# Split weights of 256 columns two to a buffer, and first weights loaded ahead of operands, in a decoder block of Strassen units

## The chip, the cores and the metric

One Trainium2 chip, one of its cores. The metric is the device time of one launch in microseconds (us).

## The reference

A decoder block on 2048 tokens of width 1024, in float32: RMS norm, one input projection, gated linear attention beside a gated short convolution, output projection, residual, then a SwiGLU feed-forward block (FFN) with residual, and a last norm. The change lies in the FFN, whose hidden width is 2816:

```python
h2 = rmsnorm(x, norm2_g[l])
ffn = (jax.nn.silu(h2 @ w_ffn_gate[l]) * (h2 @ w_ffn_up[l])) @ w_ffn_down[l]
x = x + ffn
```

## The kernel before

**Matmuls.** Activations lie transposed, channels on the 128 partitions and tokens along the row. Every float32 operand of a matmul is split in two: ACT copies the rounded high part (L153) and DVE subtracts it to get the low part (L154). A product takes three matmuls, high by high, high by low and low by high (`product_step`, L381 to L383), each 128x128 by 128x512.

**Units.** `unit` (L385) multiplies a two by two block of weights with a two by two block of activations by seven products in place of eight, after Strassen and Winograd. Its weights come in one DMA into a buffer `raw` with four quarters (A11, A12, A22, A21; `raw_weights`, L351; the pool `rawp` has two such buffers). `unit_weights` (L358) makes the other four factors from them on POOL (GpSimd): s1 (L364), A21 overwritten (L365), A11 overwritten (L366, the factor S2) and A12 overwritten (L371, S4). So the raw buffer comes free only with the last of its splits. Each of the seven factors is then split by `weight_quarter` (L345) into a buffer `wq` that holds high and low of up to 512 columns; the pool `wqp` has four such buffers, each used by one factor, whatever its width. A product keeps its buffer until its last matmul. The products run in the order A11·B11, S1·T1, S2·T2, A12·B21, S3·T3, S4·B22, A22·T4, on PSUM banks that some of them share: ACT copies a bank out (L401), DVE adds others (L405).

**FFN.** The tokens are done in two halves of 1024. For each half `ffn_up` (L904) runs 22 units of 512 columns, gate and up by turns; the operands B11, T1, T2, B21, T3, B22, T4 of the first half are in SBUF (pool `opp`, 28 buffers, tile `op`), those of the second half are loaded by `load_h2` (L895) from DRAM (`shB11_0` and so on, 512 KB each, 28 loads). Silu, the product of gate and up, and the differences that the down projection needs are split and stored to DRAM (`sa_...`). `ffn_down` (L938) takes the hidden channels in groups: the first group of two blocks with weights `wdown_first`, where a factor has 256 columns (four units, 6 matmuls for a product), the later groups of three blocks with weights `wdown` of 384 columns. Four units make one group. The first group copies its products to y (L401); later groups add theirs to y on POOL (L982), and x1, the residual, too (L989). The finished rows of the first half are stored to DRAM (`sx...`).

**Order.** The program is written in one sequence; a tile scheduler decides from it, at build time, the order of each engine's instructions, with semaphores between engines. All loads and stores are issued by SP, in order: what stands behind a waiting load or store on SP waits too. `load_h2` ties its loads behind a raw load of weights: `raw_loads[-2]`, the last but one at that point.

**The three places.** B1 is the boundary from up to down in the first half, B2 the start of the second half, B3 the boundary from up to down in the second half. The prediction uses these names.

Of the kernel before, what the change touches and what calls it, by code (L numbers as in the profile page):

```python
# [51 lines left out]
def tile_hymba_block(ctx, tc, x, xt, win, wa, wgu, wout, wffn, wdown, wdown_first, small, out):  # L52
# [188 lines left out]
    def no_operands():  # L241
        return {b: [] for _, b in PRODUCTS}
# [87 lines left out]
    def plain_unit(src, ops):  # L330
# [11 lines left out]
                us.append((r, j, settled(o, True), False))  # L342
        return us

    def weight_quarter(src):  # L345
        n = src.shape[-1]
        h = wqp.tile([P, 2, PB], F32R, name="wq", tag="wq")[:, :, 0:n]
        split(src, h[:, 0, :], h[:, 1, :])
        return h

    def raw_weights(src):  # L351
        n = src.shape[-1]
        raw = rawp.tile([P, 4 * PB], F32, name="raw", tag="raw")[:, 0 : 4 * n]
        raw = raw.rearrange("p (a n) -> p a n", a=4)
        raw_loads.append(load(raw, src))
        return raw

    def unit_weights(src):  # L358
        raw = raw_weights(src)
        n = src.shape[-1]  # L360
        a11, a12, a22, a21 = [raw[:, i, :] for i in range(4)]
        s1 = rawp.tile([P, PB], F32, name="s1", tag="s1", bufs=1)[:, 0:n]
        w = {"A11": weight_quarter(a11)}
        pool.tensor_tensor(s1, a21, a22, ALU.add)  # L364
        pool.tensor_tensor(a21, a11, a21, ALU.subtract)  # L365
        pool.tensor_tensor(a11, s1, a11, ALU.subtract)  # L366
        w["S1"] = weight_quarter(s1)
        w["S2"] = weight_quarter(a11)
        w["A12"] = weight_quarter(a12)
        w["S3"] = weight_quarter(a21)  # L370
        pool.tensor_tensor(a12, a12, a11, ALU.subtract)  # L371
        w["S4"] = weight_quarter(a12)
        w["A22"] = weight_quarter(a22)
        return w
# [7 lines left out]
        pe.matmul(o[:], wh, xl, start=False, stop=False, skip_group_check=True)  # L382
        return pe.matmul(o[:], wl, xh, start=False, stop=k == n - 1, skip_group_check=True)  # L383

    def unit(src, ops, into=None):  # L385


        w = unit_weights(src)

        def mul(i, o=None):  # L390
            first = o is None
            o = bank() if first else o
            n, m = PRODUCTS[i]
            for k in range(len(ops[m])):
                product_step(o, w[n], ops[m], k, first)
            tick()
            return o

        def copied(name, o, at):
            t = tt(name) if into is None else into[at]  # L400
            act.activation(t[:], o[:], AF.Copy)  # L401
            return t

        def plus(t, o):
            dve.tensor_tensor(t[:], o[:], t[:], ALU.add)  # L405
            return t


        oa = mul(0)
        c11 = copied("c11", oa, (0, 0))  # L410
        ob = mul(1)
        c22 = copied("c22", ob, (1, 1))
        mul(2, oa)
        c12 = copied("c12", oa, (0, 1))
        plus(c11, mul(3))
        mul(4, oa)
        plus(c22, oa)
        mul(5, ob)
        plus(c12, ob)
        mul(6, oa)  # L420
        if into is not None:
            copied("c21", oa, (1, 0))
        return [(0, 0, c11, False), (1, 1, c22, False), (0, 1, c12, False), (1, 0, oa, True)]
# [469 lines left out]
        yield from combine(lambda k, j: s_x1[2 + j][k][:], C_G2, rb, put)  # L893

    def load_h2():  # L895
        ops, loads = no_operands(), raw_loads[-2]
        for _, n in PRODUCTS:
            for k in range(4):
                o = opp.tile([P, 2, PB], F32R, name="op", tag="op")
                with tc.issue_after(loads.ins):  # L900
                    load(o[:].bitcast(F32), s_h2p[n][k][:])
                ops[n].append(o)
        return ops

    def ffn_up(half, ops):
        for m in range(NF // 2):
            us = unit(wffn[2 * m], ops)
            sg = {(r, j): silu(c, p) for r, j, c, p in us}
            for r, j, c, _ in unit(wffn[2 * m + 1], ops):
                s = sg[r, j]  # L910
                dve.tensor_tensor(s[:], c[:], s[:], ALU.mult)
            b11, b12, b21, b22 = [sg[r, j] for r in range(2) for j in range(2)]
            t1, t2, t3, t4 = [bt(n) for n in ("t1", "t2", "t3", "t4")]
            for y, p, q in ((t1, b12, b11), (t2, b22, t1), (t3, b22, b12), (t4, b21, t2)):
                pool.tensor_tensor(y[:], p[:], q[:], ALU.subtract)
            values = [("B11", b11), ("B21", b21), ("B22", b22)]
            if half == 1 and m >= LAST_GROUP:
                values.append(("B12", b12))
            values += [("T1", t1), ("T2", t2), ("T3", t3), ("T4", t4)]
            background.insert(0, split_later(s_act[half][m], values))  # L920
# [17 lines left out]
    def ffn_down(half):  # L938

        y, early = {}, {}  # L940

        def group_op(m, n):
            return early.pop((m, n)) if (m, n) in early else act_op(half, m, n)

        for u, m0 in enumerate(GROUPS):
# [10 lines left out]
            for d0 in range(0, KD, 2):  # L956
                src = wdown[4 * u - 4 + d0 // 2] if u else wdown_first[d0 // 2]
                if u == 0 and d0 == 2:

                    order = [(m, n) for _, n in PRODUCTS for m in range(GROUPS[1], GROUPS[2])]  # L960
                    for m, n in order[:EARLY]:
                        early[m, n] = act_op(half, m, n)
                if u == 0:
                    for d in (d0, d0 + 1):
                        if d < KD - 1:
                            pair = opp.tile([P, 2, PB], F32, name="y", tag="op")
                        for j in range(2):
                            y[d, j] = pair[:, j, :] if d < KD - 1 else bt("y")[:]
                    unit(src, ops, {(r, j): y[d0 + r, j] for r in range(2) for j in range(2)})
                    continue  # L970
                xs = []
                if u < 3:
                    for d in (d0, d0 + 1):
                        xs.append((y[d, u - 1], bt("x1")))
                        load(xs[-1][1][:], s_x1[2 * half + u - 1][d][:])
                if last and half and d0 == KD - 2:
                    last_unit(src, ops, [act_op(half, m, "B12") for m in ms], y, ssq)
                    break
                for r, j, c, p in unit(src, ops):
                    yy = y[d0 + r, j]  # L980
                    eng = dve if p or last and half and r != j else pool
                    eng.tensor_tensor(yy, c[:], yy, ALU.add)  # L982
                    if last and half:
                        sum_squares(ssq[j], yy, j not in begun)
                        begun.add(j)
                    elif last:
                        store(s_x1[2 * half + j][d0 + r][:], yy)
                for yy, x1 in xs:
                    pool.tensor_tensor(yy, x1[:], yy, ALU.add)  # L989
# [107 lines left out]
        ctx.enter_context(tc.tile_pool(name=n, bufs=bufs, reuse_waits="tile"))  # L1097
        for n, bufs in (("fx", 11), ("fo", 3))
    ]
    for half in range(2):  # L1100
        ffn_up(half, load_h2() if half else h2)
        ffn_down(half)
    drain_background()
    for _ in ahead[0]:
        pass
# [103 lines left out]
```

## Time and profile before

| | us |
|---|---|
| median of three runs | 2098.65 |
| the three runs | 2102.15, 2098.65, 2098.31 |
| the profiled execution's own time | 2102.39 |
| span of its profile | 2100.5 |
| mean granted TensorE clock | 0.992 |

| engine | busy, share of the span |
|---|---|
| PE (TensorE) | 97% |
| DVE (VectorE) | 68% |
| ACT (ScalarE) | 48% |
| POOL (GpSimd) | 46% |

The profile is one execution, read by a hardware profiler. A row of a timeline gives the start in us from the span's start, the duration, the engine, the line of the kernel, the operation, output and inputs, the shape, how many such instructions follow one another, and in brackets how long the engine had idled before and what ended it. PEld is TensorE's weight load, which runs beside its matmuls; SPq is SP's queue, where only issues of DMAs are seen. A row of the windows gives, for a stretch of time, its length, the busy time of PE, PEld, DVE, ACT and POOL with the number of instructions, the granted clock (1.00 is full), the busy share of the DMA engines and the GB/s that they moved. An instruction that hangs over a window's edge is counted in both.

### The profile page before, as it was taken

What the parts mean: (1) busy time and instruction counts of PE and PEld (TensorE: products, weight loads), DVE (VectorE), ACT (ScalarE), POOL (GpSimd) and SP (SyncE); (2) the same over time, 40 slices, a digit from 0 to 9 for tenths busy, and PEclk for the clock granted to TensorE, in tenths of its full rate; (3) what the DMA queues carried; (4) which work ended last, traced back from release to release, by engine and by line L of the source; (5) the groups of instructions that cost most, each with busy time, mean ns of one, the idle gap of its engine ahead of it and who ended that gap; (6) DMA issues with size and microseconds to landing.
All of it is one profiled execution on the core that took longest, in us unless ns stands there. A gap on an engine that the chain in (4) does not pass through costs nothing.

```text
span 2100.5 us, 26873 instructions
## 1 busy us (share of the span) xinstructions
PE 2034.6 (97%) x9133; PEld 1649.8 (79%) x9133; DVE 1420.2 (68%) x1983; ACT 1003.2 (48%) x1990; POOL 971.9 (46%) x703
## 2 busy tenths in 40 slices
PE   6999999999999999999999999999999999999996
PEld 4768888877888878788888878787888888877774
DVE  7669786549743786788887665555767766665554
ACT  6555455656542345545545443333545444453344
POOL 3436322222102464465464338774655445436764
PEclk9999999999999999999999999999999999999998
DMA  7359495425686873655646687698444554587673
GB/s 279 129 167 318 128 340 158 149 81 167 205 281 236 325 251 105 236 200 214 223 175 220 236 314 269 234 344 321 159 178 165 192 210 174 213 340 271 259 270 110
DMA packets 189241, 464.43 MB, mean 221 GB/s; under 512 B 19824, under 2 KB 65072, under 8 KB 179504
## 3 DMA queue, kind: packets, MB, share of 16 engines
q1 hardware_dynamic: 189104, 462.72, 61.1%
q8 instruction: 72, 1.18, 0.2%
q14 instruction: 65, 0.53, 0.1%
HBM read 297.49 MB, written 165.15 MB: 220 GB/s over the span
## 4 chain that ended last, share of the span: by engine, by line
PE 74%; DVE 10%; DMA 8%; issue 3%; POOL 3%; ACT 3%; SPq 0%; DVEq 0%; POOLq 0%; ACTq 0%
PE mm L381 22%; PE mm L383 22%; PE mm L382 22%; DVE wq L154 2%; DVE h L508 2%; PE mm L812 1%; DVE op L154 1%; PE mm L813 1%; PE mm L815 1%; DVE so L154 1%; DMA raw<-in_wffn_dram 1%; DMA raw<-in_wdown_dram 1%; DMA op<-shT 1%; PE a_ps L576 1%; DVE c L405 1%
## 5 line engine op out<-in xcount | busy, mean ns | idle before, releaser
L381 PE MATMUL mm<-op,wq 128*128 128x512 f32 x2499 | 981.6, 395 | 17.8 <-ACT wq L153 7.4
L382 PE MATMUL mm<-op,wq 128*128 128x512 f32 x2499 | 976.9, 391 | 0.0
L383 PE MATMUL mm<-op,wq 128*128 128x512 f32 x2499 | 966.4, 392 | 10.4 <-DVE wq L154 9.6
L154 DVE TENSOR_TENSOR wq<-raw,wq 128x512 fp32r<-128x512 f32 (+2 forms) x626 | 527.7, 850 | 333.2 <-ACT wq L153 330.4
L153 ACT ACTIVATE wq<-raw 128x512 fp32r<-128x512 f32 (+2 forms) x626 | 363.5, 587 | 548.6 <-PE mm L383 391.5
L381 PEld LDWEIGHTS mm<-op,wq 128*128 128x128 f32 x2499 | 471.1, 189 | 132.0 <-ACT wq L153 13.5
L383 PEld LDWEIGHTS mm<-op,wq 128*128 128x128 f32 x2499 | 471.1, 189 | 121.2 <-DVE wq L154 22.6
L382 PEld LDWEIGHTS mm<-op,wq 128*128 128x128 f32 x2499 | 471.1, 189 | 97.0 <-issue 1.0
L366 POOL TENSOR_TENSOR raw<-s,raw 128x512 f32<-128x512 f32 (+2 forms) x97 | 127.6, 1316 | 422.6 <-DVE wq L154 402.5
L405 DVE TENSOR_TENSOR c<-mm,c 128x512 f32<-128x512 f32 x267 | 183.0, 685 | 94.4 <-PE mm L383 92.1
L364 POOL TENSOR_TENSOR s<-raw 128x512 f32<-128x512 f32 (+2 forms) x97 | 129.4, 1334 | 205.3 <-DMA raw<-in_wffn_dram 98.7
L371 POOL TENSOR_TENSOR raw<-raw 128x512 f32<-128x512 f32 (+2 forms) x97 | 126.8, 1307 | 129.6 <-DVE wq L154 122.4
L401 ACT ACTIVATE c<-mm 128x512 f32<-128x512 f32 x267 | 155.0, 586 | 39.0 <-PE mm L383 37.7
L794 POOL TENSOR_TENSOR ssx<-ssx,q 128x512 f32<-128x512 f32 x52 | 75.8, 1470 | 158.7 <-ACT q L793 158.5
L365 POOL TENSOR_TENSOR raw<-raw 128x512 f32<-128x512 f32 (+2 forms) x97 | 135.1, 1392 | 4.0
L982 POOL TENSOR_TENSOR y<-c,y 128x512 f32<-128x512 f32 x66 | 98.7, 1497 | 57.3 <-DVE c L405 53.2
L154 DVE TENSOR_TENSOR so<-t,so 128x512 fp32r<-128x512 f32 x100 | 90.7, 913 | 24.4 <-ACT so L153 24.0
L153 ACT ACTIVATE wq<-s 128x512 fp32r<-128x512 f32 (+2 forms) x97 | 56.8, 586 | 98.7 <-PE mm L383 86.0
L812 PE MATMUL mm<-op,wq 128*128 128x512 f32 x256 | 100.9, 395 | 0.0
L813 PE MATMUL mm<-op,wq 128*128 128x512 f32 x256 | 99.8, 390 | 0.0
L154 DVE TENSOR_TENSOR wq<-s,wq 128x512 fp32r<-128x512 f32 (+2 forms) x97 | 84.0, 866 | 17.0 <-ACT wq L153 16.4
L153 ACT ACTIVATE so<-t 128x512 fp32r<-128x512 f32 x100 | 62.5, 626 | 37.8 <-DMA sa_B<-so 16.1
(181 smaller groups left out, 1880.3 us busy)
## 6 DMA issues: line engine op xcount, KB each, us to landing
raw<-in_wffn_dram SPq DMA_DIRECT2D x44, 1024.0 KB, 6.1
sa_T<-so SPq DMA_DIRECT2D x88, 512.0 KB, 4.9
op<-sa_T SPq DMA_DIRECT2D x88, 512.0 KB, 9.4
sa_B<-so SPq DMA_DIRECT2D x69, 512.0 KB, 3.4
op<-sa_B SPq DMA_DIRECT2D x69, 512.0 KB, 9.0
raw<-in_win_dram SPq DMA_DIRECT2D x23, 1024.0 KB, 5.4
raw<-in_wdown_dram SPq DMA_DIRECT2D x24, 768.0 KB, 6.1
sx<-y SPq DMA_DIRECT2D x48, 256.0 KB, 3.3
```

What stands on the lines that cost most here:

```text
L153: last_hi[:] = [act.activation(hi, src, AF.Copy)]
L154: return dve.tensor_tensor(lo, src, hi.bitcast(F32), ALU.subtract)
L364: pool.tensor_tensor(s1, a21, a22, ALU.add)
L365: pool.tensor_tensor(a21, a11, a21, ALU.subtract)
L366: pool.tensor_tensor(a11, s1, a11, ALU.subtract)
L371: pool.tensor_tensor(a12, a12, a11, ALU.subtract)
L381: pe.matmul(o[:], wh, xh, start=first and k == 0, stop=False, skip_group_check=True)
L382: pe.matmul(o[:], wh, xl, start=False, stop=False, skip_group_check=True)
L383: return pe.matmul(o[:], wl, xh, start=False, stop=k == n - 1, skip_group_check=True)
L401: act.activation(t[:], o[:], AF.Copy)
L405: dve.tensor_tensor(t[:], o[:], t[:], ALU.add)
L812: pe.matmul(o[e, j][:], wh, m[:, 0, :], start=k == 0, stop=False)
```

## The change

It has three parts and adds or removes no matmul, split, addition or transfer.

1. `weight_quarter` gives a whole `wq` buffer only to factors of more than 256 columns. Narrower ones, which only the first group of the down projection has, go two to a buffer; the second half of a buffer is kept in `beside` for the next narrow factor, across units too.
2. `ffn_down` loads the first weights of its first group at its start, ahead of the operands of that group.
3. The first gate weights of the second half are loaded ahead of `load_h2`, whose 28 operand loads are now tied behind the last raw load, which is that one.

The loop over the two halves is written out.

```diff
@@ -342,9 +342,19 @@
                 us.append((r, j, settled(o, True), False))
         return us
 
+    beside = []
+
     def weight_quarter(src):
         n = src.shape[-1]
-        h = wqp.tile([P, 2, PB], F32R, name="wq", tag="wq")[:, :, 0:n]
+        if n > PB // 2:
+            beside.clear()
+            h = wqp.tile([P, 2, PB], F32R, name="wq", tag="wq")[:, :, 0:n]
+        elif beside:
+            h = beside.pop()
+        else:
+            both = wqp.tile([P, 2, PB], F32R, name="wq", tag="wq")
+            beside.append(both[:, :, PB // 2 : PB // 2 + n])
+            h = both[:, :, 0:n]
         split(src, h[:, 0, :], h[:, 1, :])
         return h
 
@@ -355,8 +365,8 @@
         raw_loads.append(load(raw, src))
         return raw
 
-    def unit_weights(src):
-        raw = raw_weights(src)
+    def unit_weights(src, raw=None):
+        raw = raw_weights(src) if raw is None else raw
         n = src.shape[-1]
         a11, a12, a22, a21 = [raw[:, i, :] for i in range(4)]
         s1 = rawp.tile([P, PB], F32, name="s1", tag="s1", bufs=1)[:, 0:n]
@@ -382,10 +392,10 @@
         pe.matmul(o[:], wh, xl, start=False, stop=False, skip_group_check=True)
         return pe.matmul(o[:], wl, xh, start=False, stop=k == n - 1, skip_group_check=True)
 
-    def unit(src, ops, into=None):
-
-
-        w = unit_weights(src)
+    def unit(src, ops, into=None, raw=None):
+
+
+        w = unit_weights(src, raw)
 
         def mul(i, o=None):
             first = o is None
@@ -893,7 +903,7 @@
         yield from combine(lambda k, j: s_x1[2 + j][k][:], C_G2, rb, put)
 
     def load_h2():
-        ops, loads = no_operands(), raw_loads[-2]
+        ops, loads = no_operands(), raw_loads[-1]
         for _, n in PRODUCTS:
             for k in range(4):
                 o = opp.tile([P, 2, PB], F32R, name="op", tag="op")
@@ -902,9 +912,9 @@
                 ops[n].append(o)
         return ops
 
-    def ffn_up(half, ops):
+    def ffn_up(half, ops, raw=None):
         for m in range(NF // 2):
-            us = unit(wffn[2 * m], ops)
+            us = unit(wffn[2 * m], ops, raw=None if m else raw)
             sg = {(r, j): silu(c, p) for r, j, c, p in us}
             for r, j, c, _ in unit(wffn[2 * m + 1], ops):
                 s = sg[r, j]
@@ -938,6 +948,7 @@
     def ffn_down(half):
 
         y, early = {}, {}
+        raw = raw_weights(wdown_first[0])
 
         def group_op(m, n):
             return early.pop((m, n)) if (m, n) in early else act_op(half, m, n)
@@ -966,7 +977,8 @@
                             pair = opp.tile([P, 2, PB], F32, name="y", tag="op")
                         for j in range(2):
                             y[d, j] = pair[:, j, :] if d < KD - 1 else bt("y")[:]
-                    unit(src, ops, {(r, j): y[d0 + r, j] for r in range(2) for j in range(2)})
+                    into = {(r, j): y[d0 + r, j] for r in range(2) for j in range(2)}
+                    unit(src, ops, into, raw if d0 == 0 else None)
                     continue
                 xs = []
                 if u < 3:
@@ -1097,9 +1109,11 @@
         ctx.enter_context(tc.tile_pool(name=n, bufs=bufs, reuse_waits="tile"))
         for n, bufs in (("fx", 11), ("fo", 3))
     ]
-    for half in range(2):
-        ffn_up(half, load_h2() if half else h2)
-        ffn_down(half)
+    ffn_up(0, h2)
+    ffn_down(0)
+    raw = raw_weights(wffn[0])
+    ffn_up(1, load_h2(), raw)
+    ffn_down(1)
     drain_background()
     for _ in ahead[0]:
         pass
```

Line numbers behind the first part grow by 10: L381, L401 and L405 become L391, L411 and L415.

Up to B1 every engine's order is as before. What moves there on ACT, at the end of the second and the start of the third unit of the first down group. `raw_11028` before and `raw_11021` now is the third unit's weights, `y` are copies of the second unit's products, `so` are splits of activations on their way to DRAM. Before:

```order
L401 ACTIVATE y_10821<-mm_10850 128x512
L153 ACTIVATE wq_10952<-raw_10930 128x256
L153 ACTIVATE wq_10955<-raw_10930 128x256
L401 ACTIVATE y_10928<-mm_10958 128x512
L153 ACTIVATE so_10984<-t2_10785 128x512
L401 ACTIVATE y_10929<-mm_10958 128x512
L153 ACTIVATE so_11003<-t3_10786 128x512
L153 ACTIVATE wq_11031<-raw_11028 128x256
L153 ACTIVATE wq_11037<-s1_11030 128x256
```

Now:

```order
L153 ACTIVATE wq_10946<-raw_10927 128x256
L411 ACTIVATE y_10926<-mm_10963 128x512
L411 ACTIVATE y_10823<-mm_10847 128x512
L411 ACTIVATE y_10925<-mm_10951 128x512
L153 ACTIVATE wq_11024<-raw_11021 128x256
L153 ACTIVATE wq_11032<-raw_11021 128x256
L153 ACTIVATE wq_11024<-s1_11023 128x256
L411 ACTIVATE y_10926<-mm_10951 128x512
L153 ACTIVATE so_10977<-t2_10785 128x512
L153 ACTIVATE wq_11032<-raw_11021 128x256
```

The split of the third unit's A11 stood behind the copy of the second unit's last product and a split of activations; it now stands ahead of both, and two factors share a buffer (`wq_11024`).

On SP at the same place, before:

```order
L145 DMA op_10926<-sa0_2_T2_241 128x1024
L148 DMA sa0_10_B21_302<-so_10884 128x1024
L148 DMA sa0_10_B22_303<-so_10902 128x1024
L145 DMA raw_11028<-in_wdown_first_dram 128x1024
L148 DMA sa0_10_T1_304<-so_10965 128x1024
L145 DMA raw_11111<-in_wdown_first_dram 128x1024
```

Now:

```order
L145 DMA op_10923<-sa0_2_T2_241 128x1024
L145 DMA raw_11021<-in_wdown_first_dram 128x1024
L148 DMA sa0_10_B21_302<-so_10881 128x1024
L148 DMA sa0_10_B22_303<-so_10899 128x1024
L148 DMA sa0_10_T1_304<-so_10958 128x1024
```

The third unit's raw load went ahead of two stores of activations. B3 moves in the same way.

On SP at B2, the start of the second half, before (`shB11` are the four parts of the operand B11, `sx` rows of the first half, stored and reloaded as `y` for the last norm):

```order
L145 DMA op_12651<-shB11_0_412 128x1024
L148 DMA sx0_1_169<-y_10821 128x512
L148 DMA sx1_3_179<-y_10929 128x512
L148 DMA sx1_2_178<-y_10928 128x512
L148 DMA sx0_3_171<-y_10929 128x512
L145 DMA op_12653<-shB11_1_413 128x1024
L145 DMA y_12810<-sx0_1_169 128x512
L145 DMA y_12902<-sx0_2_170 128x512
L145 DMA op_12655<-shB11_2_414 128x1024
L145 DMA op_12657<-shB11_3_415 128x1024
L145 DMA y_12962<-sx0_3_171 128x512
L145 DMA raw_12707<-in_wffn_dram 128x2048
```

Now:

```order
L148 DMA sx0_3_171<-y_10926 128x512
L145 DMA y_12948<-sx0_3_171 128x512
L145 DMA raw_12637<-in_wffn_dram 128x2048
L145 DMA op_12639<-shB11_0_412 128x1024
L148 DMA sx0_4_172<-y_11019 128x512
L145 DMA op_12641<-shB11_1_413 128x1024
L145 DMA op_12643<-shB11_2_414 128x1024
L145 DMA op_12645<-shB11_3_415 128x1024
L148 DMA sx1_4_180<-y_11019 128x512
L145 DMA op_12647<-shT1_0_416 128x1024
```

The four loads of B11 stood ahead of the first gate weights of the second half and now stand behind them, around two stores.

## The prediction

> **What bounds the kernel now.** I read the page first, then TensorE's waits, then windows about each place where the order of instructions changes, and last the timelines of single engines there.
>
> The page, busy time by engine and the chain of waits:
>
> ```profile
> PE 2034.6 (97%) x9133; PEld 1649.8 (79%) x9133; DVE 1420.2 (68%) x1983; ACT 1003.2 (48%) x1990; POOL 971.9 (46%) x703
> ...
> PE 74%; DVE 10%; DMA 8%; issue 3%; POOL 3%; ACT 3%; SPq 0%; DVEq 0%; POOLq 0%; ACTq 0%
> ```
>
> TensorE is busy for 97% of the span and the change takes no matmul away. So it can only win the time in which TensorE waits, or runs slower than it can. What TensorE waits for in the Strassen units most (us in total, times, longest):
>
> ```profile
> PE mm L383 <- DVE wq L154: 9.6, 7, 2.7
> PE mm L381 <- ACT wq L153: 7.4, 7, 1.8
> PE mm L381 <- ACT c L401: 6.6, 7, 2.6
> ```
>
> These three are 24 us in the whole program; the change reaches only those at three boundaries. Windows (length; PE, PEld, DVE, ACT, POOL busy with counts; granted clock; DMA share; GB/s) give an undisturbed stretch, the first boundary from up to down (B1), the start of the second half (B2), the second boundary from up to down (B3), the stage behind B3, and parts of them:
>
> ```profile
> 1100.00:1180.00 80.00, 80.00 (x355) 66.24 (x354) 55.48 (x71) 41.10 (x73) 37.02 (x26) 1.00 0.46 165
> 1205.57:1240.99 35.42, 32.99 (x134) 25.45 (x132) 23.52 (x38) 16.85 (x38) 14.75 (x16) 0.95 0.74 286
> 1423.76:1467.12 43.36, 40.12 (x166) 31.81 (x165) 19.40 (x25) 15.71 (x27) 16.55 (x13) 0.96 0.84 332
> 1850.03:1893.79 43.76, 41.27 (x175) 32.02 (x174) 32.43 (x51) 23.17 (x52) 18.57 (x20) 1.00 0.84 325
> 1893.79:1938.69 44.90, 43.07 (x187) 34.44 (x186) 23.94 (x33) 15.67 (x31) 28.52 (x24) 1.00 0.73 269
> 1215.09:1230.69 15.60, 13.19 (x56) 9.71 (x54) 9.40 (x17) 6.40 (x15) 3.52 (x5) 1.00 0.85 328
> 1232.30:1235.80 3.50, 3.50 (x10) 2.68 (x10) 1.79 (x4) 1.70 (x5) 2.65 (x4) 0.55 0.62 250
> 1457.60:1461.00 3.40, 3.40 (x9) 2.60 (x9) 2.67 (x3) 1.24 (x3) 1.27 (x1) 0.54 0.71 239
> 1876.40:1879.80 3.40, 3.40 (x16) 2.73 (x16) 2.67 (x5) 2.52 (x6) 2.55 (x4) 1.00 0.73 300
> ```
>
> The first row sets the floor: 80.00 us for 354 weight loads (one for each matmul) is 0.226 us a matmul. A window's length less its count times 0.226 is what is lost there: B1 35.42 − 132 × 0.226 = 5.6 us, B2 6.1, B3 4.4, the stage behind B3 2.9. Together that is 19 us, the most that these places hold. The profiled execution took 2102.39 us (span 2100.5, so 1.9 around it), 3.74 more than the median of 2098.65, so a gain read from it may hold terms that the median runs don't have.
>
> **The waits that fall.** TensorE's timeline at the boundaries (start, duration, what ended the idle time ahead):
>
> ```profile
> 1227.51 0.50 PE L381 MATMUL mm<-op,wq 128*128 128x512 f32 x1 [0.79 <-DVE y L405]
> ...
> 1230.69 0.50 PE L381 MATMUL mm<-op,wq 128*128 128x512 f32 x1 [1.51 <-ACT wq L153]
> ...
> 1454.60 0.50 PE L381 MATMUL mm<-op,wq 128*128 128x512 f32 x1 [1.50 <-DMA op<-shT]
> ...
> 1457.25 0.74 PE L381 MATMUL mm<-op,wq 128*128 128x512 f32 x1 [1.69 <-ACT c L401]
> ...
> 1875.14 0.50 PE L381 MATMUL mm<-op,wq 128*128 128x512 f32 x1 [1.51 <-ACT wq L153]
> ...
> 1930.18 0.50 PE L381 MATMUL mm<-op,wq 128*128 128x512 f32 x1 [1.76 <-ACT wq L153]
> ```
>
> *B1.* The 1.51 us at 1230.69 is the third unit's A11 weight. Its history, read backwards on ACT, SP and DVE:
>
> ```profile
> 1211.27 0.42 ACT L153 ACTIVATE wq<-raw 128x256 fp32r<-128x256 f32 x1 [1.88 <-PE mm L383]
> ...
> 1230.23 0.41 ACT L153 ACTIVATE wq<-raw 128x256 fp32r<-128x256 f32 x1
> ```
>
> ```profile
> 1213.96 1.47 SPq L148 DMA_DIRECT2D sa_B<-so  x2
> 1216.02 0.33 SPq L145 DMA_DIRECT2D raw<-in_wdown_first_dram  x1
> ```
>
> ```profile
> 1215.01 0.95 DVE L154 TENSOR_TENSOR wq<-raw,wq 128x256 fp32r<-128x256 f32 x1
> ```
>
> ```profile
> raw<-in_wdown_first_dram SPq DMA_DIRECT2D x1, 512.0 KB, 9.6
> ```
>
> A split at 1211.27 had to wait 1.88 us for TensorE, since all four wq buffers were in use. So the first unit's last split ended at 1215.01 + 0.95 = 1215.96; only then was its raw buffer free, and the third load went out at 1216.02, behind two stores. It took 9.6 us, to 1225.6. On ACT its split, at 1230.23, stands behind the copy of the second unit's last product (the order of ACT shown with the change). With eight quarters in the four buffers all seven of a unit fit, so the first unit's splits do not wait for its products. The 1.88 is gone and the load leaves SP ahead of the two stores, by my estimate at 1216.02 less the stores' 1.47 and the wait's 1.88, so 1212.7, landing 9.6 later, 1222.3; and the order puts the split ahead of the copy. What is late next is only the 0.79 wait at 1227.51, a DVE addition between two products on one bank: it is in no buffer's hands and I leave it. The price of the 1.51 wait: the wait itself, a refill, and the clock behind it. Refill: in 1215.09 to 1230.69 15.60 − 54 × 0.226 = 3.4 us are lost and 15.60 − 13.19 = 2.4 are idle, so 1.0 goes to slower matmuls about two waits, 0.5 each. Clock: 0.55 over 3.50 us is 0.45 × 3.50 = 1.6. The term: 1.51 + 0.5 + 1.6 = **3.6 faster** (bounds: 0, if the wait stays, and 4.3, if of the 5.6 only the 0.79 and its 0.5 stay).
>
> The third unit's operands are those of the first, so no load of theirs is pushed behind it. The first raw load of the group, now written ahead of the operands, costs nothing by my estimate: it also waits for a buffer that a split sets free (bounds ±0.33, the time of one issue on SP in the row of 1216.02).
>
> *B3.* The same wait of 1.51 at 1875.14, yet the clock stays at 1.00 behind it (last window row): 1.51 + 0.5 = **2.0 faster** (bounds 0 and 3.1, which is 4.4 less 0.79 and 0.5).
>
> *The stage behind B3, and the one behind B1.* The next groups have weights of 384 columns and lie one to a buffer, as before. POOL and ACT there:
>
> ```profile
> 1928.59 0.99 POOL L366 TENSOR_TENSOR raw<-s,raw 128x384 f32<-128x384 f32 x1
> ```
>
> ```profile
> 1282.58 1.35 ACT L153 ACTIVATE wq<-raw 128x384 fp32r<-128x384 f32 x3 [1.35 <-POOL raw L366]
> ```
>
> ```profile
> 1284.51 0.39 PE L381 MATMUL mm<-op,wq 128*128 128x512 f32 x1
> ```
>
> The 1.76 wait at 1930.18 is POOL's: S2 is made at 1928.59, at the end of additions to y that themselves wait for products. In the first half S2's split is there by about 1283.1 (a third of 1.35 after 1282.58) and wanted at 1284.51, a lead of 1.4 us. TensorE comes 2 to 3.6 us earlier at both stages; POOL comes earlier too, since its additions follow the products and its raw data lands earlier, but its chain is not shorter. I take **0** for both together (bounds: 2.3 faster, if the 1.76 and a refill go; 2.2 slower, if POOL doesn't move at all and the 3.6 outruns the 1.4).
>
> *B2.* SP's timeline, and the window up to where TensorE first waits:
>
> ```profile
> 1404.79 0.33 SPq L145 DMA_DIRECT2D raw<-in_wffn_dram  x1
> 1405.89 4.40 SPq L148 DMA_DIRECT2D sx<-y  x2
> ```
>
> ```profile
> 1423.76:1450.90 27.14, 27.10 (x119) 21.81 (x118) 10.41 (x14) 8.79 (x15) 10.07 (x7) 1.00 1.03 415
> ```
>
> The raw load now stands ahead of the four B11 loads, but it can't go before 1404.79: its buffer comes free by a split. So the raw gains nothing, and four loads of 512 KB that had gone out before it, now follow. Behind it the DMA engines are full (share 1.03, 415 GB/s), so 512 KB take 1.26 us, and four 5.1. Against that, SP stood 4.40 us at 1405.89 in stores that waited for POOL; in the new order B11 loads stand there. I take 5.1 − 4.4 = **0.7 slower**, where TensorE already waits for a load, at 1454.60 (the op<-shT row above); bounds 0 and 5.1. The next wait, 1.69 at 1457.25, is ACT's copy behind a silu that wants the last product; it moves along, with its slow clock.
>
> **Sum.** 3.6 + 2.0 + 0 − 0.7 = 4.9 faster: the profiled 2102.39 would be 2097.5, and the median 2098.65 − 4.9 = **2093.8**, if the median runs carry the clock's 1.6 at B1 as this one does. The forecast's own range is 2092.3 to 2094.9. A difference within 0.2% (4.2 us, so from 2094.45 to 2102.85) can't be told from no change here.
>
> **The rivals.**
>
> *The clock's 1.6 does not hang on the wait.* For it: the same 1.51 wait is followed by 0.55 at 1232.30 and by 1.00 at 1876.40. Then B1 is 2.0 and the whole 3.3: 2095.4. The Trainium skill ("TensorE: Matmul & The Clock Gate", Part 1: The HAM clock gate) has the clock halve only after at least one idle window of about 3.4 us; by that, waits of 1.5 us would cost no clock and the sum would be this rival's. The trace does not bear it out as told: 0.55 stands behind waits of 0.79 and 1.51, and 0.54 behind 1.50 and 1.69, with no wait of 3.4 near.
>
> *POOL takes the place of the weights.* Both stages behind the boundaries give back what TensorE gained over the 1.4 lead: 2.2 of B1's. 4.9 − 2.2 = 2.7: 2096.0. For it: POOL's order is not made shorter and the 1.76 wait is already there.
>
> *More.* The 1.76 wait and its refill go with the earlier raw load: 4.9 + 2.3 = 7.2: 2091.4. For it: in the trace POOL's work on that raw stands between its additions; an earlier landing lets it run before them.
>
> *The pairing gives no room,* since a buffer comes free only when both its quarters were used; the third load stays at 1216.02. Only B2's 0.7 is left: 2099.4. Against it: the order of SP shows the load ahead of both stores.
>
> *Slower: the B11 loads at B2.* If SP's hole isn't filled, since the loads wait for landings that the raw load delays, all 5.1 come at 1454.60, with 0.5 of refill and another slow-clock stretch of 0.46 × 3.40 = 1.6: 7.2 in place of 0.7, so 5.6 − 7.2 = 1.6 slower, 2100.2; with POOL's 2.2 also given back, 2102.4, and beyond 2102.85 if B3 fails too. It ends slower than before from the point where B2 loses over 5.6 us. Against it: the hole of 4.40.
>
> **Chances.** The forecast 0.44, the clock 0.12, POOL 0.14, more 0.12, no room 0.06, slower 0.12 (most of it beyond 0.2%, since what fails there tends to fail together: its 2100.2 is with B1 and B3 whole). Faster by over 0.2%: 0.8 of the forecast and all of more, so 0.47; slower by over 0.2%: three quarters of the last, 0.09; within 0.2%: the rest, 0.44. The range takes in more (with 1.4 of the 0.7 and 1.1 left in B1 and B3, 2090.0) and the slower case's first step: 2090.0 to 2100.5, which leaves out 0.1 or a little more.
>
> **What would show it.** Right: the third load of the first down group issued near 1212.7, no wait for ACT's wq at the third unit of B1 and B3, the clock at 1.00 behind B1, and a wait for op<-shT at B2 under 2.5 us. Wrong: a wait for POOL's S2 (or S1) of over 2 us in the stages behind; B11 loads that go out only after 1410.3 (1405.89 + 4.40); a slow-clock stretch that only moved elsewhere.

## The result, and the profile after

The changed kernel took 2098.53 us (median of 22 runs, 2093.91 to 2103.42) against 2102.96 for the kernel before (22 runs). The ratio is 0.9974, 95% interval 0.9967 to 0.9981: 5.5 us faster (4.0 to 6.9). This ratio is not the quotient of the two medians, which differ by 4.4; both 4.4 and the forecast of 4.9 us (ratio 0.9977) lie inside the interval. The forecast's 2093.8 was counted from the median of the three runs known then, 2098.65, and over 22 runs the kernel before stands 4.3 higher, so the difference is to be compared and not the absolute time.

Its page, busy time by engine:

```profile
PE 2031.8 (97%) x9133; PEld 1649.6 (79%) x9133; DVE 1411.9 (67%) x1983; ACT 1001.9 (48%) x1990; POOL 973.5 (46%) x703
```

The counts are the same, and TensorE is again busy for 97%. What TensorE waits for in the units (total, times, longest):

```profile
PE mm L393 <- DVE wq L154: 12.3, 12, 3.0
PE mm L391 <- ACT c L411: 6.6, 7, 2.6
PE mm L391 <- ACT wq L153: 5.7, 5, 1.9
```

These were 9.6, 6.6 and 7.4: in this pair of executions the sum went up by 1. The gain is thus not in the total of this view, and the same stretches of the program have to be compared. Windows of the changed kernel between the same matmuls: B1, the stage behind it, B2, B3 and the stage behind that; then the 3.5 us behind B1 and a slow stretch in B2:

```profile
1207.20:1238.90 31.70, 30.65 (x134) 24.66 (x133) 21.53 (x38) 16.74 (x39) 15.41 (x17) 1.00 0.79 308
1238.90:1349.07 110.17, 108.55 (x472) 87.79 (x471) 60.31 (x83) 39.19 (x78) 77.05 (x62) 1.00 0.70 266
1422.77:1467.07 44.30, 39.91 (x167) 31.60 (x165) 19.23 (x25) 15.70 (x27) 17.19 (x13) 0.96 0.88 344
1850.40:1891.50 41.10, 40.04 (x175) 32.50 (x174) 28.41 (x49) 22.23 (x50) 19.02 (x20) 1.00 0.86 331
1891.50:1937.70 46.20, 43.53 (x187) 34.50 (x186) 21.69 (x32) 15.43 (x31) 28.91 (x24) 1.00 0.75 281
1230.70:1234.20 3.50, 3.50 (x17) 2.87 (x16) 2.15 (x5) 3.27 (x9) 2.59 (x3) 1.00 0.17 71
1440.20:1443.60 3.40, 3.37 (x9) 2.70 (x10) 0.00 (x0) 0.00 (x0) 2.38 (x2) 0.59 1.03 408
```

The stage behind B1 had not been shown for the kernel before; its row there:

```profile
1240.99:1350.08 109.09, 108.08 (x472) 87.95 (x471) 60.31 (x85) 40.38 (x81) 77.37 (x62) 1.00 0.72 265
```

Lost time is again a window's length less 0.226 us for each weight load:

| stretch | lost before | lost after | difference |
|---|---|---|---|
| B1 | 5.6 | 1.6 | −4.0 |
| behind B1 | 2.6 | 3.7 | +1.1 |
| B2 | 6.1 | 7.0 | +0.9 |
| B3 | 4.4 | 1.8 | −2.6 |
| behind B3 | 2.9 | 4.2 | +1.3 |

Both boundaries won about what was forecast, 6.6 together, and half as much, 3.3, was lost in the stages that follow. TensorE's timeline shows where:

```profile
1219.03 0.50 PE L393 MATMUL mm<-op,wq 128*128 128x512 f32 x1 [0.27 <-DVE wq L154]
...
1229.23 0.50 PE L391 MATMUL mm<-op,wq 128*128 128x512 f32 x1 [0.78 <-DVE y L415]
...
1318.11 0.50 PE L391 MATMUL mm<-op,wq 128*128 128x512 f32 x1 [1.40 <-ACT wq L153]
...
1439.07 0.50 PE L391 MATMUL mm<-op,wq 128*128 128x512 f32 x1 [1.86 <-ACT wq L153]
...
1456.12 0.50 PE L391 MATMUL mm<-op,wq 128*128 128x512 f32 x1 [0.49 <-DMA op<-shT]
...
1923.85 0.50 PE L393 MATMUL mm<-op,wq 128*128 128x512 f32 x1 [1.37 <-DVE wq L154]
...
1929.38 0.50 PE L391 MATMUL mm<-op,wq 128*128 128x512 f32 x1 [1.10 <-ACT wq L153]
```

At B1 the 0.78 wait is left, and a short one of 0.27 is new. Behind B1 there is one of 1.40, at B2 one of 1.86 for the second (up) weights, behind B3 a new one for DVE beside that for ACT. On SP and ACT at B1 the changed kernel has:

```profile
1214.72 0.33 SPq L145 DMA_DIRECT2D raw<-in_wdown_first_dram  x1
1216.97 1.47 SPq L148 DMA_DIRECT2D sa_B<-so  x2
```

```profile
1226.26 0.72 ACT L153 ACTIVATE wq<-raw 128x256 fp32r<-128x256 f32 x2
...
1230.92 0.60 ACT L411 ACTIVATE y<-mm 128x512 f32<-128x512 f32 x1 [3.64 <-PE mm L393]
```

This execution enters B1 1.7 us later than that of before, so the third load at 1214.72 is 3.0 us earlier than the one at 1216.02 (3.3 forecast). The split (1226.26) stands ahead of the copy that waits 3.64 us for TensorE (1230.92).

### The profile page after: what moved, and what is told of

The parts are those of the page before. It is cut to its first block, busy times and chain, and to the rows that moved or that the text cites. A ratio compares the mean times of both kernels' runs of the same rounds, so it can differ in the third digit from the quotient of the medians.

```text
span 2098.3 us, 26852 instructions
## 1 busy us (share of the span) xinstructions
PE 2031.8 (97%) x9133; PEld 1649.6 (79%) x9133; DVE 1411.9 (67%) x1983; ACT 1001.9 (48%) x1990; POOL 973.5 (46%) x703
## 4 chain that ended last, share of the span: by engine, by line
PE 74%; DVE 7%; DMA 5%; POOL 2%; issue 2%; ACT 2%; SPq 0%; DVEq 0%; POOLq 0%; ACTq 0%
PE mm L391 22%; PE mm L393 22%; PE mm L392 22%; DVE wq L154 2%; PE mm L822 2%; PE mm L823 2%; PE mm L825 2%; DVE so L154 1%; DVE h L518 1%; DMA raw<-in_wdown_dram 1%; DMA op<-shT 1%; DMA raw<-in_wffn_dram 1%; DMA op<-sa_T 1%; PE o_ps L746 1%; PE o_ps L748 1%
## 5 line engine op out<-in xcount | busy, mean ns | idle before, releaser
L391 PE MATMUL mm<-op,wq 128*128 128x512 f32 x2499 | 980.9, 394 | 15.0 <-ACT c L411 6.6
L154 DVE TENSOR_TENSOR wq<-raw,wq 128x512 fp32r<-128x512 f32 (+2 forms) x626 | 519.3, 837 | 312.4 <-ACT wq L153 310.1
L391 PEld LDWEIGHTS mm<-op,wq 128*128 128x128 f32 x2499 | 470.8, 188 | 128.0 <-ACT wq L153 11.0
L415 DVE TENSOR_TENSOR c<-mm,c 128x512 f32<-128x512 f32 x267 | 183.0, 686 | 101.5 <-PE mm L393 99.5
L381 POOL TENSOR_TENSOR raw<-raw 128x512 f32<-128x512 f32 (+2 forms) x97 | 126.5, 1304 | 131.4 <-DVE wq L154 124.0
L411 ACT ACTIVATE c<-mm 128x512 f32<-128x512 f32 x267 | 154.9, 585 | 28.7 <-PE mm L393 27.4
```

The costliest lines, as they stand in the source:

```text
L154: return dve.tensor_tensor(lo, src, hi.bitcast(F32), ALU.subtract)
L391: pe.matmul(o[:], wh, xh, start=first and k == 0, stop=False, skip_group_check=True)
```

## The experiments

The first four and the next four ran beside the kernel before; the last two repeat two of them.

| kernel | ratio to before, 95% |
|---|---|
| changed kernel | 0.9974 (0.9967 to 0.9981) |
| early load of the down weights alone | 0.9996 (0.9986 to 1.0006) |
| pairing alone | 0.9968 (0.9957 to 0.9979), again 0.9972 (0.9962 to 0.9983) |
| early load of the gate weights alone | 1.0001 (0.9993 to 1.0010) |
| changed kernel, x1 added on DVE | 0.9961 (0.9949 to 0.9973), again 0.9972 (0.9961 to 0.9982) |
| copy tied behind the split, nothing else | 0.9988 (0.9979 to 0.9996) |
| two pairs of seven factors | one run, 2096.15 us |
| kernel before, x1 added on DVE | 0.9997 (0.9988 to 1.0005) |
| pairing alone, x1 added on DVE | 0.9974 (0.9963 to 0.9985) |

The ratios carry about ±0.001 (2 us). The traces tell more: the time from the first to the last matmul of each stretch, less that of the same matmuls in the profile of the kernel before, in us:

| profile of | B1 | behind B1 | B2 | B3 | behind B3 |
|---|---|---|---|---|---|
| changed kernel | −3.8 | +1.1 | +0.9 | −2.7 | +1.3 |
| early down weights alone | 0.0 | 0.0 | +1.9 | 0.0 | 0.0 |
| pairing alone | −3.9 | +0.2 | +0.6 | −2.6 | +1.3 |
| the same again | −3.8 | +0.8 | +1.2 | −2.7 | +1.2 |
| early gate weights alone | −1.6 | 0.0 | +1.0 | +2.0 | −0.4 |
| changed kernel, x1 on DVE | −3.8 | +0.2 | +1.1 | −2.6 | −0.5 |
| the same again | −3.8 | −0.6 | +1.1 | −2.6 | −0.6 |
| copy behind the split | −3.7 | +0.2 | +1.6 | −2.0 | +1.9 |
| two pairs of seven | −4.4 | +0.2 | +2.2 | −3.2 | −1.0 |
| before, x1 on DVE | 0.0 | −0.6 | +0.6 | +1.6 | −1.5 |
| pairing alone, x1 on DVE | −3.8 | −0.6 | −1.2 | −2.6 | −0.5 |

Where a stretch is the same program in two rows it agrees to about 0.1, but for slow stretches of the clock (1.6 each, most of the scatter in B2) and the stage behind B1.

**The early load of the down weights alone.** Part 2 of the change on the kernel before.

```diff
         y, early = {}, {}
+        raw = raw_weights(wdown_first[0])
...
+                    unit(src, ops, into, raw if d0 == 0 else None)
```

> Only the second part of the change: the first weights of the down projection are loaded ahead of its operands. The built order of every engine is that of the kernel before. Theory (the room in the split buffers does it): nothing moves, ratio to before 1.000 within the interval; the trace has TensorE waiting about 1.5 us for the third unit's weight at the first and the second boundary from up to down. Rival (the earlier load does part of it): 0.5 us or more faster at each boundary. On the clock: if the slow stretch behind the first boundary hangs on the wait alone, it is there again (a granted clock near 0.55 over 3.4 us); if the wait only sometimes brings it, it may be missing.

It is 0.9996, no difference. The scheduler had already put this load where its buffer comes free. As it is the kernel before over again, its trace serves for the clock: TensorE's row at B1, and the window behind it.

```profile
1227.48 0.50 PE L381 MATMUL mm<-op,wq 128*128 128x512 f32 x1 [1.51 <-ACT wq L153]
```

```profile
1228.20:1231.60 3.40, 3.37 (x10) 2.63 (x10) 2.01 (x4) 1.54 (x5) 2.56 (x3) 0.55 0.70 288
```

The wait of 1.51 recurs to the hundredth, at B3 too, with the slow clock behind it at B1 and not at B3.

**The pairing alone.** Part 1 of the change on the kernel before.

```diff
+        if n > PB // 2:
+            beside.clear()
+            h = wqp.tile([P, 2, PB], F32R, name="wq", tag="wq")[:, :, 0:n]
+        elif beside:
+            h = beside.pop()
+        else:
...
```

> Only the first part: weights of 256 columns two to a buffer. Theory (room): the whole gain of both boundaries, 2.0 to 3.8 us at the first and 2.7 at the second, about 1 us given back behind each, and the start of the second half as before, without the 0.9 us that the trace of the changed kernel loses there: ratio to before 0.997, as good as the whole change or 0.0005 better. Rival (the earlier loads do it): 0.999 or above, with a wait for the third unit's weight over 1 us at a boundary.

0.9968, so the theory holds: the pairing alone gains as much as the whole change. Neither boundary has a wait for the third unit's weights. Behind B3 its waits are those of the changed kernel:

```profile
1919.29 0.50 PE L393 MATMUL mm<-op,wq 128*128 128x512 f32 x1 [1.37 <-DVE wq L154]
1921.84 0.50 PE L393 MATMUL mm<-op,wq 128*128 128x512 f32 x1 [0.21 <-DVE wq L154]
1924.82 0.50 PE L391 MATMUL mm<-op,wq 128*128 128x512 f32 x1 [1.10 <-ACT wq L153]
```

Behind B1, however, TensorE waits 0.47 where the changed kernel, with the same order there, waited 1.40: that loss is not fixed. So it was repeated.

> The pairing alone, once more. Theory (the earlier gate weights of the second half cost about what they change, 0.3 us in waits): ratio to before 0.9965 to 0.9975, not to be told from the changed kernel's 0.9974; TensorE's waits of 1.5 us at the two boundaries are gone and no slow stretch of the clock stands behind them. Rival (they cost as first feared, more than 1 us): below 0.9965.

0.9972, with 1.08 behind B1. The gate weights' part can't be told from nothing by the times.

**The early load of the gate weights alone.** Part 3 on the kernel before.

```diff
-        ops, loads = no_operands(), raw_loads[-2]
+        ops, loads = no_operands(), raw_loads[-1]
...
+    raw = raw_weights(wffn[0])
+    ffn_up(1, load_h2(), raw)
```

> Only the third part: the first gate weights of the second half are loaded ahead of its operands. Theory (it costs): at the start of the second half TensorE waits near 1.9 us for the second (up) weights, which now stand behind two operand loads more, and about 1 us less for op<-shT later: 0.5 to 1.5 us slower there, ratio 1.0003 to 1.0007, inside the noise; both boundaries from up to down as before, with their waits of 1.5. Rival (it gains): the start of the second half 1 us or more faster, ratio 0.9995 or less.

1.0001, which doesn't tell the theory's loss from nothing. Its trace has the wait for the second weights, and 1.51 at both boundaries:

```profile
1231.79 0.50 PE L381 MATMUL mm<-op,wq 128*128 128x512 f32 x1 [1.51 <-ACT wq L153]
...
1439.34 0.50 PE L381 MATMUL mm<-op,wq 128*128 128x512 f32 x1 [1.62 <-ACT wq L153]
...
1876.42 0.50 PE L381 MATMUL mm<-op,wq 128*128 128x512 f32 x1 [1.51 <-ACT wq L153]
```

No wait for op<-shT follows. So part 3 moves a wait from the operands at the end of B2 to the second weights. The clock behind the two waits of 1.51 here:

```profile
1232.60:1236.00 3.40, 3.40 (x15) 2.77 (x16) 2.66 (x5) 2.00 (x5) 2.60 (x3) 1.00 0.73 298
1876.90:1880.30 3.40, 3.37 (x10) 2.44 (x9) 1.91 (x4) 1.44 (x5) 2.57 (x3) 0.57 0.64 261
```

The other way round than in the kernel before: full at B1, slow at B3.

**The additions of x1 on DVE.** On the changed kernel; the x1 rows are the residual, added in the second group of each half.

```diff
-                    pool.tensor_tensor(yy, x1[:], yy, ALU.add)
+                    (dve if u == 1 else pool).tensor_tensor(yy, x1[:], yy, ALU.add)
```

> The changed kernel with the eight additions of the residual x1 to y in the second group of each half's down projection moved from POOL to DVE. Theory (what is given back behind the boundaries is POOL's long chain of additions): the waits of 1.4 us (behind the first boundary) and 1.4 and 1.1 us (behind the second) fall to under 1 us together: 2 to 3 us faster than the changed kernel, ratio to before 0.996. Rival (the given-back time hangs on the DMA stream of operand loads and on the order of DVE): the waits stay within 0.5 us, or move to DVE's splits, ratio 0.997 to 0.998.

The wait for S2 behind B3 is gone, DVE's of 1.37 falls to 0.80, and its short one of 0.21 becomes 0.36:

```profile
1920.26 0.50 PE L393 MATMUL mm<-op,wq 128*128 128x512 f32 x1 [0.80 <-DVE wq L154]
1922.97 0.50 PE L393 MATMUL mm<-op,wq 128*128 128x512 f32 x1 [0.36 <-DVE wq L154]
```

That is 1.37 + 0.21 + 1.10 = 2.68 of waits down to 1.16, and the stage goes from +1.3 to −0.5; behind B1 it goes from a mean of +0.7 (the changed kernel and the two of pairing alone) to +0.2. So POOL's chain of additions costs more in these two stages than the change gave back there; whether the change is what made it cost that much, the same edit on the kernel before has to say (below). The ratio was 0.9961, and repeated:

> The changed kernel with the eight additions of x1 on DVE, once more. Theory (1.8 us less behind the second boundary in the trace is a gain of the time too): ratio to before 0.9955 to 0.9970, below the changed kernel's 0.9974. Rival (the slow stretches of the clock, which come and go between runs, swallow it): 0.9970 to 0.9980.

0.9972, as its rival had it, though the trace repeats the gain (−0.6 behind both boundaries). These 2 to 3 us are 0.001 to 0.0015, which the intervals don't resolve: they are shown in the traces and not in the time.

**The copy behind the split.** The kernel before; only the place of one copy on ACT is forced.

```diff
+    late = []
...
         w = {"A11": weight_quarter(a11)}
+        while late:
+            t, o = late.pop()
+            with tc.issue_after(last_hi[0].ins):
+                act.activation(t[:], o[:], AF.Copy)
...
-            copied("c21", oa, (1, 0))
+            late.append((into[1, 0], oa))
```

> The kernel before, with no pairing and no earlier load: only the copy of a first-group unit's last product (to y) is tied on ACT behind the A11 split of the unit that follows. The third raw load stays behind the two stores. Theory A (the 1.51 us wait is ACT's order alone: the raw data land at 1225.6, 3.6 us ahead of the need at 1229.2): both waits of 1.51 fall to under 0.3, 2.0 to 2.7 us at each boundary, ratio to before about 0.998 after what is given back behind them. Theory B (the earlier raw load is needed): the wait at the third unit stays over 1 us at both boundaries, because POOL's and DVE's work on the raw data is then late, ratio 0.9995 to 1.0005.

Its SP and ACT at B1, and TensorE behind B3:

```profile
1219.47 1.47 SPq L148 DMA_DIRECT2D sa_B<-so  x2
1221.53 0.33 SPq L145 DMA_DIRECT2D raw<-in_wdown_first_dram  x1
```

```profile
1231.34 0.42 ACT L153 ACTIVATE wq<-raw 128x256 fp32r<-128x256 f32 x1 [0.68 <-DMA raw<-in_wdown_first_dram]
1234.72 0.60 ACT L369 ACTIVATE y<-mm 128x512 f32<-128x512 f32 x1 [2.96 <-PE mm L389]
```

```profile
1908.94 0.50 PE L387 MATMUL mm<-op,wq 128*128 128x512 f32 x1 [1.25 <-ACT wq L153]
1910.12 0.50 PE L389 MATMUL mm<-op,wq 128*128 128x512 f32 x1 [0.45 <-DVE wq L154]
...
1933.59 0.50 PE L387 MATMUL mm<-op,wq 128*128 128x512 f32 x1 [1.86 <-ACT wq L153]
```

The third load still goes out behind the two stores, 10.45 us after the entry into B1 as in the kernel before, and the split no longer waits for anything but its data (1231.34, ahead of the copy at 1234.72). The 1.51 is gone at both boundaries, and B1 gains 3.7 of pairing's 3.8. Theory A holds: it was the order on ACT, not the late load. B3 gains 2.0 of pairing's 2.6, and behind it waits of 1.25 and 0.45 come up and 1.86 stays: 0.9988 in all. There the raw load of the second unit of 384 columns went out late:

```profile
1898.86 0.33 SPq L145 DMA_DIRECT2D raw<-in_wdown_dram  x1
```

That is 45.3 us after the entry into B3, against 35.0 in the changed kernel and 41.8 in the kernel before. So a part of what this kernel loses behind B3 can be the price of the forced place itself; no run separates it from the missing room.

**Two pairs of seven.** The pairing alone, with A11, S1 and A22 in a buffer of their own.

```diff
+        if n > PB // 2 or alone:
...
+        w = {"A11": weight_quarter(a11, True)}
...
+        w["S1"] = weight_quarter(s1, True)
...
+        w["A22"] = weight_quarter(a22, True)
```

> Only the first part of the change, at a smaller dose: of the seven factors of 256 columns S2 with A12 and S3 with S4 share a buffer, A11, S1 and A22 have one each, so a unit takes five buffers of the four in place of four. Theory (room decides by how early a unit's last split is done): the third raw load goes out between that of before (12.0 us ahead of the first need of the third unit's weights at 1228.1 less waits) and that of the changed kernel, and the wait for its first weight is gone as with full pairing, since the order on ACT is the same at that place; small waits for DVE's low parts of 0.2 to 0.6 us may appear. Rival (all seven must fit): the waits of 1.5 us are there as before.

At B1 there is only the 0.79 wait, and none at the third unit:

```profile
1224.52 0.50 PE L391 MATMUL mm<-op,wq 128*128 128x512 f32 x1 [0.79 <-DVE y L415]
```

Part of the room is enough for the wait, and B1 and B3 even gain more than with full pairing, 0.6 each. That is the 0.27 wait (0.26 to 0.29), which every kernel with full pairing has at both boundaries and this one at neither: matmul by matmul, the pairing alone falls 0.54 us behind this kernel at that wait in B1 and 0.55 in B3, and hardly anywhere else in them. TensorE waits there for the low part of the second unit's A11. DVE starts it 10.8 us after the entry into B1 in the changed kernel (first row), and 9.4 us after it here:

```profile
1218.02 0.96 DVE L154 TENSOR_TENSOR wq<-raw,wq 128x256 fp32r<-128x256 f32 x1
```

```profile
1212.61 0.96 DVE L154 TENSOR_TENSOR wq<-raw,wq 128x256 fp32r<-128x256 f32 x1
```

The third load, expected between that of before and that of the changed kernel, went out at 1209.86, earlier than both, counted from the entry into B1 (6.7 us after it, against 10.4 and 7.4). A later stage gave 2.7 back, with a wait of 1.51 and a slow stretch at 1959, so that one run, 2096.15, says nothing of the whole.

**x1 on DVE without the pairing.** The same edit as above on the kernel before.

> The kernel before, with only the eight additions of x1 in the second group of each half moved from POOL to DVE. Theory (the 1.76 us wait behind the second boundary is POOL's chain, with or without the pairing): it falls to under 0.9, and the boundaries keep their waits of 1.5: 1 to 2.5 us faster, ratio 0.9990 to 0.9995. Rival (POOL's chain only decides after the pairing has moved TensorE forward): nothing beyond 0.5 us, ratio 1.000.

The wait behind B3 falls from 1.76 to 0.40, so POOL's chain set it before the change too:

```profile
1933.72 0.50 PE L381 MATMUL mm<-op,wq 128*128 128x512 f32 x1 [0.40 <-ACT wq L153]
```

Behind both boundaries the trace gains (0.6 and 1.5), as the theory had it; the ratio, 0.9997, doesn't separate it from the rival. This weakens the reading of POOL above: set beside this kernel, the three profiles with the pairing and x1 on DVE (mean −0.3 and −0.5) still give back 0.3 behind B1 and 1.0 behind B3, of the 0.7 and 1.3 without it. So about 0.7 of the 2.0 is POOL's, by one profile, whose slow stretch at B3 can move the stage behind it too. At both boundaries it has the 1.51, and this time the slow clock behind both:

```profile
1234.40:1237.80 3.40, 3.40 (x10) 2.62 (x9) 2.13 (x4) 1.51 (x4) 2.54 (x4) 0.51 0.76 308
1879.30:1882.70 3.40, 3.38 (x10) 2.63 (x10) 2.00 (x4) 1.53 (x5) 2.57 (x3) 0.55 0.71 288
```

**The pairing and x1 on DVE, without the early gate weights.**

> The first part of the change alone (weights of 256 columns two to a buffer) together with the eight additions of x1 on DVE. Theory: the gains add, 6.6 us of the pairing alone (0.9968) and 1.8 to 2.6 behind the second boundary: ratio to before about 0.9958, and no wait of 1.9 us at the start of the second half, so 0.5 to 1 us better than the changed kernel with those additions on DVE (0.9961). Rival (the start of the second half waits the same in all, under another name): no better than 0.9961.

0.9974, no better, as the rival had it. At B2 TensorE waits for the operands what the changed kernel waits for the weights:

```profile
1447.40 0.50 PE L391 MATMUL mm<-op,wq 128*128 128x512 f32 x1 [1.59 <-DMA op<-shT]
```

Its profile, with no slow stretch from 152 to 2025 us, spans 2088.2, the shortest here, and its twelve runs lie between 2089.89 and 2103.16. No version is shown to beat the changed kernel.

## Why the prediction was right

**B1 (3.6 forecast, 3.8 in the trace).** The terms hold: the 1.51 is gone, with refill and slow clock. The reason was half right. The forecast named the earlier load and the order on ACT together; the copy tied behind the split shows that the order alone removes the wait. What the room adds to that, by the same experiment, is 0.1 at B1, 0.6 at B3 and 0.6 behind B3, if the forced place costs nothing itself. Full pairing also pays 0.5 at each boundary for the 0.27 wait, which the forecast did not have.

**B3 (2.0 forecast, 2.7 in the trace).** The wait went; the 0.6 that the copy behind the split does not bring came with it, within the bound of 3.1.

**Behind the boundaries (0 forecast, 2.4 slower in this pair).** This term was mis-sized: 2.4 is beyond the forecast's own bound of 2.2, and the mean of the three profiles with this order is 2.0 (0.7 and 1.3). The forecast's reason for the bound, POOL's chain, holds in part. S2 in the first half does come late in the changed kernel: TensorE's weight loads wait 0.33 and 0.34 for it at 1282.49 and 1283.60, which cost 0.4, and none of the kernels with x1 on DVE has that. The largest wait there, 1.40, has another place. The raw data of a later unit came late,

```profile
1307.26 0.33 SPq L145 DMA_DIRECT2D raw<-in_wdown_dram  x1
```

issued at 1307.26 and 10.2 us to landing, in a full stream of operand loads (DMA share 1.03 until then). Counted from the start of the stage this load goes out after 65.4 us in the kernel before, 67.4 to 68.4 in the changed kernel and the pairing alone, and 65.6 to 66.7 with x1 on DVE, so POOL's additions have a part in that too. The wait was 0.61 in the kernel before, 1.40 in the changed one, and 0.47 and 1.08 in the two profiles of the pairing alone: it differs between executions of one program. Behind B3 POOL's wait for S2 fell, from 1.76 to 1.10. What is lost there is DVE's part (1.37), a low part of A11 queued behind an addition that waits for the previous unit's last product, and it was not foreseen:

```profile
1922.07 0.69 DVE L994 TENSOR_TENSOR y<-mm,y 128x512 f32<-128x512 f32 x1 [1.35 <-PE mm L393]
1922.68 1.12 DVE L154 TENSOR_TENSOR wq<-raw,wq 128x384 fp32r<-128x384 f32 x1
```

**B2 (0.7 slower forecast, 0.9 in the trace).** The size was about right, the place wrong. B11 came in time, its loads going out from 1404.17 to 1406.9. The second raw load slid behind two more operand loads instead:

```profile
1426.92 0.33 SPq L145 DMA_DIRECT2D raw<-in_wffn_dram  x1
```

It took 11.4 us from there, hence the 1.86 at 1439.07; and op<-shT, waited for by 1.50 before, now costs 0.49. Summed over all waits at B2, four profiles with part 3 (changed kernel, part 3 alone, x1 on DVE twice) have 3.7 to 4.4 us, mean 4.1; eight without it have 3.2 to 4.2, mean 3.7. Its cost is about 0.3 in waits. B2's slow stretch did not go; in the changed kernel it stands behind the 1.86.

**The clock.** The rival that the 1.6 does not hang on the wait is refuted. Over all profiles the pattern of 0.78 and 1.51 at a boundary was there 8 times (four kernels with both boundaries) and a slow stretch followed in 5; without the 1.51 there were 16 boundaries (eight profiles) and it followed in none. So the term is no 1.6 at B1 and 0 at B3, as the one trace had it, but 5/8 × 1.6 = 1.0 at each; these two sums are nearly the same by luck.

Which of the eight are followed can be read from the traces. In all twelve profiles the granted clock changes only on a grid of 3.413 us: the slow stretches of the kernel before start at 784.91, 1232.06, 1457.34 and 2037.61, which are 131, 66 and 170 times 3.413 us apart. Where the grid lies differs between executions. Windows laid on it, of the kernel before, two at B1 and two at B3:

```profile
1228.65:1232.06 3.41, 1.88 (x8) 0.92 (x7) 1.70 (x4) 2.24 (x5) 0.52 (x1) 1.00 0.43 174
1232.06:1235.47 3.41, 3.41 (x10) 2.63 (x9) 2.04 (x4) 1.51 (x4) 2.56 (x4) 0.50 0.71 287
...
1870.35:1873.76 3.41, 2.49 (x10) 1.42 (x8) 1.56 (x3) 0.10 (x1) 1.35 (x2) 1.00 0.41 166
1873.76:1877.18 3.42, 2.02 (x8) 1.37 (x9) 2.37 (x4) 2.20 (x6) 1.12 (x2) 1.00 0.51 210
```

At B1 the wait lies whole in one such window, which has only 0.92 us of weight loads, and the clock is 0.50 for the whole of the next. At B3 an edge cuts the wait, both windows have more (1.42 and 1.37), and nothing follows. The five that were followed have 0.92 to 0.95 us of weight loads in the window of the wait; of the three that weren't two are cut by an edge, and none has under 1.05. The same holds for all such windows at full clock in the twelve profiles, without the first 200 us and the last 30: with up to 0.95 us of weight loads all 28 were followed by a slow one, from 1.04 to 1.2 us 2 of 9, above that none of some 6480. So the 0.78, which lies a window earlier in these five, has no part in it, and 5 in 8 is how often the wait lay so on the grid.

The Trainium skill ("TensorE: Matmul & The Clock Gate", Part 1: The HAM clock gate) wants an idle window of about 3.4 us for the slow clock. Here 1.53 us without a matmul in such a window was enough, so the measurement decides against that as far as idle means without any work.

**The sum.** Against the mean of the four profiles that have the waits (B1 −0.4 and B3 +0.9 in the table, with the kernel before as 0): B1 3.8 − 0.4 = 3.4, B3 2.7 + 0.9 = 3.6, less 0.7 behind B1, 1.3 behind B3 and 0.3 at B2: 4.7 faster, inside the measured 4.0 to 6.9. That it lies so near the forecast's 4.9 is luck in part: B3 brought 1.6 more than forecast (0.9 of it the clock's), and the stages behind took 2.0 that were forecast as 0. The single pair of profiles differs by only 2.2 in span: its five stretches sum to 3.2 less, B3's slow stretch was not in that of before, and the changed kernel's execution enters B1 1.7 late, up to where both programs are the same.

The rival that the pairing gives no room, and the slower one, are refuted by the third load at 1214.72 and by B11 in time. "More" did not happen: the 1.76 became 1.37 and 1.10. The rival of POOL had the size of what is given back, 2.2, nearly right; but behind B3 it was DVE in the main, and its total of 2.7 missed what B3 gained more.

What stays open: what decides on the clock between 1.04 and 1.2 us of weight loads in a window, and how much of the time behind B3 each of POOL, DVE and the room has.

## What to carry to other kernels

When a change moves buffers under a scheduler, look at what it moves on the in-order engines: here a split that stood behind a copy waiting for TensorE was the wait, and tying the copy later without any buffers removed the same 1.51 us. Gains at a boundary are partly given back in the next stage by the next engine in line (POOL and DVE here), so price that stage too and not only the wait that goes; and run the edit that is to explain a loss on the kernel before as well, since a gain there too explains less of it. A slow-clock stretch behind a wait in one trace is a term with a probability, because the wait falls elsewhere on the clock's grid in the next execution, and only several profiles give it.

## What the runs showed of the hardware

The granted clock changed only on a grid of 3.413 us, which lay elsewhere in each of the twelve executions, and between the first 200 us and the last 30 it stood at 0.50 for one such window or two. What came ahead was a window with little work for TensorE: all 28 with up to 0.95 us of weight loads (an undisturbed one has 66.24 / 80 × 3.41 = 2.8) were followed by a slow one, and none of some 6480 with over 1.2 us. So a wait of 1.51 us, equal to 0.01 us in every profile that has it, was followed by the slow clock in 5 of 8 cases, at a price of about 1.6 us.

The same kernel in other runs spans 10 us (2098.31 to 2107.76 for the kernel before), about six such stretches of 1.6. They explain a part of it: among the 25, 29 and 15 runs of the kernel before that stand beside the experiments, a lower mean clock goes with a longer time (correlation 0.77, 0.28 and 0.58); how large a part was not measured.
